# Three Strassen-like pairs instead of two in gate/up blocks 1 to 5, with two pairs' remainders built by adding transfers

## The chip, the cores and the metric

The kernel runs on one core of a Trainium2 chip. The metric is the device time of the program in microseconds (us). The engines are TensorE (PE; its weight loads are PEld), VectorE (DVE), ScalarE (ACT), GpSimd (POOL) and SyncE (SP, which here only issues transfers).

## The reference, cut to what matters

One decoder layer on 256 tokens of width 2048, in float32. The change touches only the first product of the two feed-forward parts.

```python
def swiglu(x, w_gate, w_up, w_down):
    return (jax.nn.silu(x @ w_gate) * (x @ w_up)) @ w_down
x = x + 0.5 * swiglu(rms_norm(x, ffn1_norm), ffn1_w_gate, ffn1_w_up, ffn1_w_down)   # D_FF = 5632
...  # attention and gated linear attention between two projections
x = x + 0.5 * swiglu(rms_norm(x, ffn2_norm), ffn2_w_gate, ffn2_w_up, ffn2_w_down)
```

## The kernel before, in words

**Numbers in two parts.** TensorE multiplies in a short format (fp32r). Every float32 operand W is therefore split: ACT copies it to `wh` (the rounded head), DVE subtracts `wl = W - wh` (the remainder). A product is three matmuls: head by head, remainder by head, head by remainder. The activations, `hh` and `hl`, are split once.

**Gate/up.** The 5632 columns go in 11 blocks of 512 gate and 512 up columns. In each, the 16 k-tiles of 128 rows come as eight *k-pairs*; a k-pair's weights are one transfer of 1 MB into a buffer `raw` (three buffers in rotation, issued on SP). A *plain* pair (letter `s`) costs 2 k-tiles x 2 token halves x 2 column groups x 3 = 24 matmuls of 128x512. A pair *by seven products* (letter `g`) uses Strassen's scheme with 7 products x 3 = 21 matmuls, and needs sums of weights, which DVE makes: `plain` (a sum and a split), `last` (`swh`, `swl`), `sums` (two additions, a split) and `more` (a split). `FF_ORDERS` gives the pairs' order: blocks 1 to 10 have `ssgssgss`, block 0 has `ssssssss`. The split weights lie in four buffers `wh`, `wl` (`WBUF`); `weights()` prepares up to three ahead.

**Around a block.** `evac` takes a block's results out of PSUM (two subtractions and additions `sg`, ACT's silu, a product `u`, a transpose `us`), and 32 small transfers on POOL's queue (`move_squares`, "moves") turn it. `finish`, which comes one block later, splits the turned result into `uh`, `ul`, the input of the down product. `fold` adds the seven-product banks together. `later` spreads such pieces over the plain pairs.

**What sets the order.** Each engine runs its own queue strictly in order. The queue is made at build time: a scheduler with a time model of its own reorders the program, so that it is not the order of the source.

Of the kernel before, what the change touches and what calls it, by code (L numbers as in the profile page):

```python
# [14 lines left out]
F32 = mybir.dt.float32  # L15
F32R = mybir.dt.float32r
U32 = mybir.dt.uint32
AF = mybir.ActivationFunctionType
ALU = mybir.AluOpType
AX = mybir.AxisListType  # L20

P = 128
S = 256
D = 2048
FF = 5632
# [5 lines left out]
FF_SEVEN = range(1, 11)  # L31
# [7 lines left out]
def _order(text):  # L39

    seven, plain = iter(range(text.count("g"))), iter(range(text.count("g"), len(text)))
    return [(next(seven), True) if c == "g" else (next(plain), False) for c in text]


FF_ORDERS = [_order("ssgssgss" if b in FF_SEVEN else "ssssssss") for b in range(FF // 512)]
DOWN_ORDERS = [_order("ssssssgssgssgsgsgsgsss"), _order("sgsssgssgssgssgsgsssss")]
OUT_ORDERS = [_order("ssssssss"), _order("ssgsgsss")]

# [1 line left out]
def layer_kernel(tc, x, xT, gains, gla_gate_up, gla_gate_bias, gla_out_norm, att_q_norm, att_k_norm,  # L50
                 w_ff1, w_dn1, w_mix, w_low, w_out, w_ff2, w_dn2, c_sq, c_rope, c_mask, out):

    nc = tc.nc
# [3 lines left out]
    with ExitStack() as es:  # L57
        cst = es.enter_context(tc.tile_pool(name="cst", bufs=1))
        wp = es.enter_context(tc.tile_pool(name="wp", bufs=2))
# [3 lines left out]
        order = [0]  # L63
# [109 lines left out]
            rsqrt(rt[:, t:t + 1], ssum[:, t:t + 1])  # L173


        def jobs_of(w, orders):
            for cp, order in enumerate(orders):
                for kp, seven in order:
                    for part in ("plain", "last", "sums", "more") if seven else (0, 1):
                        yield w, cp * len(order) + kp, part  # L180

        jobs = [*jobs_of(w_ff1, FF_ORDERS), *jobs_of(w_dn1, DOWN_ORDERS)]
        jobs += [(w_mix, i, k) for i in range(3 * KT // 2) for k in range(2)] + ["low"]
        jobs += [(w_mix, i, k) for i in range(3 * KT // 2, 3 * KT) for k in range(2)]
        jobs += jobs_of(w_out, OUT_ORDERS)
        jobs += [*jobs_of(w_ff2, FF_ORDERS), *jobs_of(w_dn2, DOWN_ORDERS)]

        AHEAD = 2
        ready = []
# [6 lines left out]
        def prepare():  # L196
            if not jobs:
                return
            job = jobs.pop(0)
            if job == "low":  # L200
                raw = wp.tile([P, KT, P], F32, name="raw", tag="raw", bufs=3)
                nc.sync.dma_start(raw, w_low.rearrange("p (k f) -> p k f", f=P))
                got = []
                for i in range(2):
                    w = wtile("wh").rearrange("p j f -> p (j f)").rearrange("p (k f) -> p k f", f=P)
                    nc.vector.memset(w.bitcast(F32), 0.0)
                    split(w[:, :, 0:RANK], w[:, :, 64:64 + RANK], raw[:, 8 * i:8 * i + 8, 0:RANK])
                    got.append(w)
                ready.extend(got)
                return  # L210
            w, i, k = job
            if k in ("last", "sums", "more"):
                return seven(k, w)
            if k == "plain" or k == 0:
                raw = raws[0] = wp.tile([P, 2, 2, 512], F32, name="raw", tag="raw", bufs=3)
                flat = raw.rearrange("p k j f -> p (k j f)")
                parts = 1 if started else 4
                started.append(True)
                for c in range(0, 2048, 2048 // parts):
                    nc.sync.dma_start(flat[:, c:c + 2048 // parts], w[i, :, c:c + 2048 // parts])  # L220
            if k == "plain":
                return seven(k, w)
            wh, wl = wtile("wh"), wtile("wl")
            if len(started) < 3:
                started.append(True)
                for j in range(2):
                    split(wh[:, j], wl[:, j], raws[0][:, k, j])
            else:
                split(wh, wl, raws[0][:, k])
            ready.append((wh, wl))  # L230

        rooms = {}

        def seven(part, w):

# [47 lines left out]
        later = []  # L283
# [45 lines left out]
        def seven_pair(acts, pairs, forms, odd, evac, fold, span=None, final=False):  # L329

            cs, ms, folds = [acc_bank(), acc_bank(), tp_bank(), tp_bank()] if odd is None else four_banks(odd), None, []
            if odd is not None:
                order[0] = 4 * (1 - odd)
            units = [u for kp, seven in pairs for u in ([kp] if seven else [(2 * kp,), (2 * kp + 1,)])]
            lastseven = max(n for n, u in enumerate(units) if not isinstance(u, tuple))
            steps = span or 2 * sum(isinstance(u, tuple) for u in units)
            total = done = step = n = 0  # L340
            while n < len(units):
                u = units[n]
                if isinstance(u, tuple):
                    g = WBUF if final and n == len(units) - WBUF else 1
                    ws = [weights() for _ in range(g)]
                    last = n + g == len(units)
                    for t in range(NT):
                        step += 1
                        total = max(total, done + len(later))
                        go = min(max(-(-total * min(step, steps) // steps) - done, 0), len(later))  # L350
                        done += go
                        run_later(go)
                        if folds:
                            folds.pop(0)()
                        now = [acts[v[0]] for v in units[n:n + g]]
                        products(cs[2 * t:2 * t + 2], t, now, ws, n == 0, last, ((0,), (1,)) if g > 1 else ((0, 1),))
                        if last:
                            evac(t, [c.rearrange("p (a b) -> p b a", b=2) for c in cs[2 * t:2 * t + 2]])
                    n += g
                    continue  # L360
                start = ms is None
                if start:
                    ms = [acc_bank() for _ in range(4)] if odd is None else four_banks(1 - odd)
                seven_products(cs, ms, acts[2 * u:2 * u + 2], forms[u], start, n == lastseven)
                if start:
                    later.extend(second)
                    second.clear()
                if n == lastseven:
                    folds = fold([m.rearrange("p (a b) -> p b a", b=2) for m in ms])
                    if holding[0] == 1:  # L370
                        later.extend(held)
                        held.clear()
                        holding[0] = total = done = step = 0
                        steps = 2 * (len(units) - n) - 6
                n += 1
# [35 lines left out]
        hacts = [(hh, hl, k) for k in range(KT)]  # L411

        def lent(a, k, i):

            return a[:, k:k + 2, :].rearrange("p k (t q) -> p (k t) q", q=P) if i else a[:, k:k + 2, :].rearrange("p k s -> p (k s)").unsqueeze(1)
# [15 lines left out]
        def ffn(name, done, residual, extra=None, final=False):  # L431

            with tc.tile_pool(name=name, bufs=1, reuse_waits="tile") as fp:

                tail = FT - TAIL
                us_h = [fp.tile([P, tail, S], F32R, name="uh")]
                us_l = [fp.tile([P, tail, S], F32R, name="ul")]
                spare = ExitStack()
                urs = xs[:, 0, 0:NT * 512].rearrange("p (t f) -> p t f", t=NT)
                extra_sums, tails = [], []  # L440

                def part(k):
# [3 lines left out]
                for b in range(FF // 512):  # L446
# [23 lines left out]
                    if b == FF_SEVEN[0]:  # L470
                        sp = spare.enter_context(tc.tile_pool(name=name + "s", bufs=1, reuse_waits="tile"))
                        t4 = xs[:, 1, :].rearrange("p (i f) -> p i f", i=4)
                        p1, u1, u2, u3 = [halves(t4[:, i, :]) for i in range(4)]
                        extra_sums = [u1, p1, u3, u2]
                        room = rooms["gate"] = {"sum": xs[:, 0, NT * 512:].rearrange("p (j f) -> p j f", j=2)}
                        for n in ("wh", "wl"):
                            room[n] = sp.tile([P, 1, 512], F32R, name="s" + n)
                        fs = [sp.tile([P, 2, 4, P], F32R, name="f" + n) for n in "hl"]
                        forms = {kp: [f[:, kp] for f in fs] for kp in range(2)}
                        later[:0] = [lambda kp=kp: seven_forms(hacts[2 * kp:2 * kp + 2], forms[kp], t4[:, 0, :], t4[:, 1, :]) for kp in range(2)]  # L480

                        def fold(m):
                            return [lambda: nc.scalar.activation(p1, m[0], AF.Copy),
                                    lambda: nc.vector.tensor_add(u1, p1, m[2]),
                                    lambda: nc.vector.tensor_add(u2, u1, m[3]),
                                    lambda: nc.vector.tensor_add(u1, u1, m[1]),
                                    lambda: nc.vector.tensor_add(u3, u2, m[1])]
# [500 lines left out]
```

## Time and profile before

| what | value |
|---|---|
| time, median of three runs (1716.45, 1719.28, 1719.43) | 1719.28 us |
| span of the profiled execution (the page gives no other time of it) | 1715.9 us |
| PE busy | 1705.4 us, 99% |
| DVE busy | 1416.9 us, 83% |
| ACT busy | 947.1 us, 55% |
| POOL busy | 505.7 us, 29% |
| moved by transfers | 378.62 MB, mean 221 GB/s |

The span runs from the first to the last instruction. A matmul's row shows 379 ns, since matmuls overlap in the pipeline; how fast they follow each other is read from two events whose matmuls are counted. Idle time of an engine other than PE costs something only where PE then waits.

### The profile page before, as it was taken

Reading aid. Unit: us, or ns where it says so; the run is one execution under the profiler, and the core shown is the slowest. Engines: PE = TensorE matmul, PEld = TensorE weight load, DVE = VectorE, ACT = ScalarE, POOL = GpSimd, SP = SyncE. Lnnn points to the kernel's source line nnn. Section 1 sums busy time; section 2 is a strip of 40 time slices with the busy share of each in tenths; the row PEclk is TensorE's granted clock in tenths of the full one; section 3 lists DMA queues with packets and bytes.
Section 4 is the critical chain, followed back from the end, with each engine's and each line's share of the span. In section 5 each row is a group of like instructions: output and inputs, shape, how many; then the busy total and the mean of one; then the engine's idle time right before and its main releaser. Section 6 shows DMA issues by size and latency. Waiting matters only on the chain.

```text
span 1715.9 us, 22309 instructions
## 1 busy us (share of the span) xinstructions
PE 1705.4 (99%) x7974; PEld 1485.1 (87%) x7974; DVE 1416.9 (83%) x1731; ACT 947.1 (55%) x1173; POOL 505.7 (29%) x1002
## 2 busy tenths in 40 slices
PE   9999999999999999999999999999999999999999
PEld 7888888888888888888888888888888888888887
DVE  6888889898898788577865788788888898898876
ACT  7555555555555555564654555555555555555453
POOL 0333334344410611054250043333333333420000
PEclk9999999999999999999999999999999999999999
DMA  8666666556665657577564467666666666665654
GB/s 345 213 229 224 219 211 232 208 213 236 234 250 219 217 203 244 192 237 235 195 210 172 148 198 269 210 231 225 222 224 220 226 212 224 218 242 222 248 204 147
DMA packets 85807, 378.62 MB, mean 221 GB/s; under 512 B 21392, under 2 KB 38800, under 8 KB 42688
## 3 DMA queue, kind: packets, MB, share of 16 engines
q1 hardware_dynamic: 50864, 350.25, 57.2%
q0 software_dynamic: 34112, 25.88, 5.3%
q8 instruction: 62, 1.02, 0.2%
q10 hardware_dynamic: 720, 1.07, 0.2%
q14 instruction: 49, 0.40, 0.1%
HBM read 354.57 MB, written 4.19 MB: 209 GB/s over the span
## 4 chain that ended last, share of the span: by engine, by line
PE 89%; DMA 4%; DVE 4%; POOL 1%; issue 1%; ACT 0%; DVEq 0%; SPq 0%; ACTq 0%; POOLq 0%
PE acc L279 20%; PE acc L277 20%; PE acc L281 20%; PE tp L281 4%; PE tp L277 4%; PE tp L279 4%; PE acc L303 4%; PE acc L304 4%; PE acc L302 4%; DVE wl L115 2%; DMA raw<-in_w_dn_dram 2%; DMA hh<-us 1%; PE tp L303 1%; PE tp L304 1%; PE tp L302 1%
## 5 line engine op out<-in xcount | busy, mean ns | idle before, releaser
L114 ACT ACTIVATE wh<-raw 128x1024 fp32r<-128x1024 f32 (+1 forms) x660 | 683.6, 1048 | 531.2 <-PE acc L281 186.6
L115 DVE TENSOR_TENSOR wl<-raw,wh 128x1024 fp32r<-128x1024 f32 (+1 forms) x658 | 790.3, 1215 | 168.4 <-ACT wh L114 165.0
L136 POOL DMA_DIRECT2D xs<-us x704 | 344.9, 497 | 552.1 <-ACT wh L114 200.3
L281 PE MATMUL acc<-wh,hl 128*128 128x512 f32 x1232 | 370.7, 380 | 0.0
L279 PE MATMUL acc<-wl,hh 128*128 128x512 f32 x1232 | 369.9, 380 | 0.1
L277 PE MATMUL acc<-wh,hh 128*128 128x512 f32 x1232 | 363.5, 381 | 2.6 <-ACT wh L114 2.6
L277 PEld LDWEIGHTS acc<-wh,hh 128*128 128x128 f32 x1232 | 232.3, 189 | 37.7 <-ACT wh L114 4.1
L279 PEld LDWEIGHTS acc<-wl,hh 128*128 128x128 f32 x1232 | 232.6, 189 | 33.9 <-issue 0.7
L281 PEld LDWEIGHTS acc<-wh,hl 128*128 128x128 f32 x1232 | 232.6, 189 | 32.9 <-DVE hl L544 0.2
L279 PE MATMUL acc<-wl,uh 128*128 128x512 f32 x384 | 117.2, 380 | 0.0
L281 PE MATMUL acc<-wh,ul 128*128 128x512 f32 x384 | 117.0, 379 | 0.0
L277 PE MATMUL acc<-wh,uh 128*128 128x512 f32 x384 | 112.1, 380 | 0.7 <-ACT wh L114 0.7
L136 POOL DMA_DIRECT2D hh<-us x128 | 62.4, 506 | 126.7 <-DVE us L129 69.0
L241 DVE TENSOR_TENSOR xs<-raw 128x1024 f32<-128x1024 f32 x40 | 49.0, 1225 | 46.9 <-DMA raw<-in_w_ff_dram 46.9
L277 PEld LDWEIGHTS acc<-wh,uh 128*128 128x128 f32 x384 | 72.3, 189 | 12.0 <-ACT wh L114 1.9
L279 PEld LDWEIGHTS acc<-wl,uh 128*128 128x128 f32 x384 | 72.4, 189 | 10.8 <-DVE wl L115 0.6
L281 PEld LDWEIGHTS acc<-wh,ul 128*128 128x128 f32 x384 | 72.6, 189 | 10.3
L277 PE MATMUL tp<-wh,hh 128*128 128x512 f32 x240 | 73.2, 379 | 0.0
L281 PE MATMUL tp<-wh,hl 128*128 128x512 f32 x240 | 71.4, 379 | 0.0
L279 PE MATMUL tp<-wl,hh 128*128 128x512 f32 x240 | 71.4, 379 | 0.0
L114 ACT ACTIVATE wh<-xs 128x1024 fp32r<-128x1024 f32 x40 | 42.2, 1055 | 45.2 <-PE acc L281 24.1
L114 ACT ACTIVATE swh<-raw 128x512 fp32r<-128x512 f32 x40 | 25.3, 631 | 60.6 <-DMA raw<-in_w_ff_dram 60.6
(326 smaller groups left out, 2382.3 us busy)
## 6 DMA issues: line engine op xcount, KB each, us to landing
raw<-in_w_ff_dram SPq DMA_DIRECT2D x175, 1024.0 KB, 5.0
raw<-in_w_dn_dram SPq DMA_DIRECT2D x88, 1024.0 KB, 4.9
raw<-in_w_mix_dram SPq DMA_DIRECT2D x48, 1024.0 KB, 5.0
raw<-in_w_out_dram SPq DMA_DIRECT2D x16, 1024.0 KB, 4.8
xs<-us POOLq DMA_DIRECT2D x704, 16.0 KB, 3.4
xs<-in_x_dram SPq DMA_DIRECT2D x2, 1024.0 KB, 9.8
xs<-in_x_dram POOLq DMA_DIRECT2D x2, 1024.0 KB, 5.4
hh<-us POOLq DMA_DIRECT2D x128, 16.0 KB, 3.7
```

What stands on the lines that cost most here:

```text
L114: nc.scalar.activation(dst_h, src, AF.Copy)
L115: nc.vector.tensor_sub(dst_l, src, dst_h.bitcast(F32))
L136: nc.gpsimd.dma_start(dst[32 * q:32 * q + 32, ..., r * n:(r + 1) * n], src[32 * r:32 * r + 32, ..., q * n:(q + 1) * n])
L241: nc.vector.tensor_add(room["sum"], b1, mid)
L277: nc.tensor.matmul(ps[j], lhsT=sh, rhs=alt(wh[:, j, :]), start=first and i == 0, stop=False)
L279: nc.tensor.matmul(ps[j], lhsT=sh, rhs=alt(wl[:, j, :]), start=False, stop=False)
L281: nc.tensor.matmul(ps[j], lhsT=sl, rhs=alt(wh[:, j, :]), start=False, stop=last and i == len(ws) - 1)
L302: nc.tensor.matmul(bank, lhsT=a[0], rhs=alt(ws[0][:, j, :]), start=start, stop=False)
L303: nc.tensor.matmul(bank, lhsT=a[0], rhs=alt(ws[1][:, j, :]), start=False, stop=False)
L304: nc.tensor.matmul(bank, lhsT=a[1], rhs=alt(ws[0][:, j, :]), start=False, stop=stop)
```

## The change

Blocks 1 to 5 of both gate/up products get the order `dsggdgss`: three pairs by seven products, three plain ones, and two of a new kind, `d`. A `d` pair's split is made in the previous block. A new job `far` loads the pair into `raw` as usual, ACT copies the heads `wh` and then writes `-wh` into the place of the remainder; a job `add` lets a transfer on POOL's queue add W from HBM onto it, so that `-wh + W` stands there. `take` hands the pair to the matmuls. The room for it is lent by `uh` and `ul`, k-tiles 24 to 39, which are filled only from block 6's results on; the forms of the third seven-product pair lie in k-tiles 20 and 21.

```diff
-FF_ORDERS = [_order("ssgssgss" if b in FF_SEVEN else "ssssssss") for b in range(FF // 512)]
+FF_FAR = range(1, 6)
+FF_ORDERS = [_order("dsggdgss" if b in FF_FAR else "ssgssgss" if b in FF_SEVEN else "ssssssss") for b in range(FF // 512)]
...
+        for b in FF_FAR:
+            for d, (at, to) in enumerate((((b - 1, 4), (b - 1, 6)), ((b - 1, 7), (b, 1)))):
+                ff_early.setdefault(at, []).append((b, d, "far"))
+                ff_early.setdefault(to, []).append((b, d, "add"))
...
+            if isinstance(k, str) and k[:4] == "take":
+                wh, wl = far[i]
+                ready.append((wh[:, int(k[4])], wl[:, int(k[4])]))
+                return
+            if isinstance(k, str) and k[:3] == "add":
+                nc.gpsimd.dma_start(far[i][1].rearrange("p k j f -> p (k j f)"), w[i], accum_op=ALU.add)
+                return
+            if isinstance(k, str) and k[:3] == "far":
+                raw = wp.tile([P, 2, 2, 512], F32, name="raw", tag="raw", bufs=3)
+                nc.sync.dma_start(raw.rearrange("p k j f -> p (k j f)"), w[i])
+                wh, wl = far[i] = [a.rearrange("p (k j h) s -> p k j (h s)", k=2, j=2) for a in rooms["far"][int(k[3])]]
+                for h in range(2):
+                    nc.scalar.activation(wh[:, h], raw[:, h], AF.Copy)
+                for h in range(2):
+                    nc.scalar.activation(wl[:, h], wh[:, h].bitcast(F32), AF.Copy, scale=-1.0)
+                return
...
+                rooms["far"] = [[a[0][:, k:k + 8, :] for a in (us_h, us_l)] for k in (24, 32)]
...
-                        forms = {kp: [f[:, kp] for f in fs] for kp in range(2)}
+                        forms[2] = [lent(a[0], 20, 1) for a in (us_h, us_l)]
```

The queues move with it. Line numbers after the change are 24 to 26 higher than before (L114 and L115 become L115 and L116, L241 becomes L265); L234 is the far head's copy, L236 the `-wh` copy, L231 the far load, L227 the add.

ACT's queue in block 3 of the first product before, from the silu of block 2's evac (`sg`) to the `finish` in the block's second half (`uh`; `wh<-xs` and `swh` belong to the `g` pairs):

```order
L452 ACTIVATE sg<-sg,rt 128x512
L114 ACTIVATE wh<-raw 128x1024
L114 ACTIVATE uh<-xs 128x4x128
L114 ACTIVATE wh<-raw 128x1024
L114 ACTIVATE wh<-xs 128x1024
L452 ACTIVATE sg<-sg,rt 128x512
L114 ACTIVATE wh<-raw 128x1024 x5
L114 ACTIVATE swh<-raw 128x512
L114 ACTIVATE wh<-raw 128x1024
L114 ACTIVATE wh<-xs 128x1024
L114 ACTIVATE wh<-raw 128x1024
L114 ACTIVATE uh<-xs 128x4x128
```

The same stretch after. The third row is the first `g`'s `more` copy, the fifth the second `g`'s `plain`, and the row `x2` below the second `g`'s `more` and the third `g`'s `plain`:

```order
L477 ACTIVATE sg<-sg,rt 128x512 x2
L234 ACTIVATE uh<-raw 128x1024 x2
L115 ACTIVATE wh<-raw 128x1024
L236 ACTIVATE ul<-uh 128x1024 x2
L115 ACTIVATE wh<-raw 128x1024
L115 ACTIVATE wh<-xs 128x1024
L115 ACTIVATE swh<-raw 128x512
L115 ACTIVATE wh<-raw 128x1024 x2
L115 ACTIVATE wh<-xs 128x1024
L115 ACTIVATE swh<-raw 128x512
L234 ACTIVATE uh<-raw 128x1024 x2
L115 ACTIVATE uh<-xs 128x4x128
```

Four copies of the first far pair now stand between the silu and the second `g`'s `plain`; two of the second far pair and a `finish` stand ahead of the third `g`'s `more` and the next plain pair, which come right behind the last row. So it is in blocks 1, 3 and 4 of the first product and 2, 3 and 4 of the second; in block 2 and block 1, respectively, the second far pair's copies stand behind the third `g`'s `more` and the first half of the plain pair. Block 5 has no far copies.

DVE's queue at the start of block 3 before, from the first `sg` of block 2's evac to the second one:

```order
L451 TENSOR_TENSOR sg<-acc,xs 128x512
L115 TENSOR_TENSOR wl<-raw,wh 128x1024
L453 TENSOR_TENSOR xs<-acc,xs 128x512 x2
L115 TENSOR_TENSOR wl<-raw,wh 128x1024
L454 SCALAR_TENSOR_TENSOR u<-xs,rt,sg 128x512
L115 TENSOR_TENSOR ul<-xs,uh 128x4x128
L129 STREAM_TRANSPOSE us<-u 128x4x4x32
L451 TENSOR_TENSOR sg<-acc,xs 128x512
```

And the same stretch after:

```order
L476 TENSOR_TENSOR sg<-acc,xs 128x512
L478 TENSOR_TENSOR xs<-acc,xs 128x512 x2
L273 TENSOR_TENSOR raw<-xs,raw 128x512
L116 TENSOR_TENSOR wl<-xs,wh 128x1024
L479 SCALAR_TENSOR_TENSOR u<-xs,rt,sg 128x512
L273 TENSOR_TENSOR raw<-raw 128x512
L265 TENSOR_TENSOR xs<-raw 128x1024
L130 STREAM_TRANSPOSE us<-u 128x4x4x32
L476 TENSOR_TENSOR sg<-acc,xs 128x512
```

The plain pairs' remainders that stood between the pieces of the evac have given way to the sums of the first `g` and the first addition of the second.

SP's queue in that region was one row of 81 equal loads; now far loads stand in it, and they take the same three buffers:

```order
L231 DMA raw<-in_w_ff_dram 128x2048
L244 DMA raw<-in_w_ff_dram 128x2048 x4
L231 DMA raw<-in_w_ff_dram 128x2048
L244 DMA raw<-in_w_ff_dram 128x2048 x2
L231 DMA raw<-in_w_ff_dram 128x2048
```

In block 3 the second far load waits for the buffer of the second `g`, which is free after that `g`'s last split. On POOL the adds stand in pairs, each pair behind one block's 32 moves and ahead of the next block's.

More of the change, by code (lines that the diff above doesn't have):

```diff
@@ L41, in _order @@
     seven, plain = iter(range(text.count("g"))), iter(range(text.count("g"), len(text)))
-    return [(next(seven), True) if c == "g" else (next(plain), False) for c in text]
-FF_ORDERS = [_order("ssgssgss" if b in FF_SEVEN else "ssssssss") for b in range(FF // 512)]
+    return [(next(seven if c == "g" else plain), c) for c in text]
+FF_FAR = range(1, 6)
+FF_ORDERS = [_order("dsggdgss" if b in FF_FAR else "ssgssgss" if b in FF_SEVEN else "ssssssss") for b in range(FF // 512)]
 DOWN_ORDERS = [_order("ssssssgssgssgsgsgsgsss"), _order("sgsssgssgssgssgsgsssss")]
@@ L173, in norm_finish, with jobs_of @@
             rsqrt(rt[:, t:t + 1], ssum[:, t:t + 1])
-        def jobs_of(w, orders):
+        def jobs_of(w, orders, early={}):
             for cp, order in enumerate(orders):
-                for kp, seven in order:
-                    for part in ("plain", "last", "sums", "more") if seven else (0, 1):
+                for at, (kp, kind) in enumerate(order):
+                    for b, d, part in early.get((cp, at), ()):
+                        yield w, b * len(order) + [k for k, c in orders[b] if c == "d"][d], part + str(d)
+                    for part in {"g": ("plain", "last", "sums", "more"), "s": (0, 1), "d": ("take0", "take1")}[kind]:
                         yield w, cp * len(order) + kp, part
-        jobs = [*jobs_of(w_ff1, FF_ORDERS), *jobs_of(w_dn1, DOWN_ORDERS)]
+        ff_early = {}
+        for b in FF_FAR:
+            for d, (at, to) in enumerate((((b - 1, 4), (b - 1, 6)), ((b - 1, 7), (b, 1)))):
+                ff_early.setdefault(at, []).append((b, d, "far"))
+                ff_early.setdefault(to, []).append((b, d, "add"))
+        jobs = [*jobs_of(w_ff1, FF_ORDERS, ff_early), *jobs_of(w_dn1, DOWN_ORDERS)]
         jobs += [(w_mix, i, k) for i in range(3 * KT // 2) for k in range(2)] + ["low"]
@@ L185, in layer_kernel @@
         jobs += jobs_of(w_out, OUT_ORDERS)
-        jobs += [*jobs_of(w_ff2, FF_ORDERS), *jobs_of(w_dn2, DOWN_ORDERS)]
+        jobs += [*jobs_of(w_ff2, FF_ORDERS, ff_early), *jobs_of(w_dn2, DOWN_ORDERS)]
         AHEAD = 2
@@ L230, in prepare @@
             ready.append((wh, wl))
-        rooms = {}
+        rooms, far = {}, {}
         def seven(part, w):
@@ L336, in seven_pair @@
                 order[0] = 4 * (1 - odd)
-            units = [u for kp, seven in pairs for u in ([kp] if seven else [(2 * kp,), (2 * kp + 1,)])]
+            units = [u for kp, kind in pairs for u in ([kp] if kind == "g" else [(2 * kp,), (2 * kp + 1,)])]
             lastseven = max(n for n, u in enumerate(units) if not isinstance(u, tuple))
@@ L479, in ffn @@
                         forms = {kp: [f[:, kp] for f in fs] for kp in range(2)}
-                        later[:0] = [lambda kp=kp: seven_forms(hacts[2 * kp:2 * kp + 2], forms[kp], t4[:, 0, :], t4[:, 1, :]) for kp in range(2)]
+                        forms[2] = [lent(a[0], 20, 1) for a in (us_h, us_l)]
+                        later[:0] = [lambda kp=kp: seven_forms(hacts[2 * kp:2 * kp + 2], forms[kp], t4[:, 0, :], t4[:, 1, :]) for kp in range(3)]
                         def fold(m):
```

## The prediction

> **What bounds the kernel now.** First the page's share of the span by engine, then busy time by stage: a stretch of gate/up blocks (50 to 90, 250 to 290) and one of the first down product (500 to 540). After the window stand span of the stretch, busy time (instructions) of PE, PEld, DVE, ACT, POOL, then granted clock, share of the transfer engines, GB/s.
>
> ```profile
> PE 1705.4 (99%) x7974; PEld 1485.1 (87%) x7974; DVE 1416.9 (83%) x1731; ACT 947.1 (55%) x1173; POOL 505.7 (29%) x1002
> 50.00:90.00 40.00, 40.00 (x187) 35.03 (x186) 33.03 (x36) 21.83 (x25) 15.76 (x32) 1.00 0.64 223
> 250.00:290.00 40.00, 40.00 (x187) 35.02 (x186) 35.74 (x41) 22.66 (x26) 15.69 (x32) 1.00 0.65 224
> 500.00:540.00 40.00, 38.69 (x177) 32.92 (x176) 34.34 (x36) 24.25 (x27) 0.00 (x0) 1.00 0.55 208
> ```
>
> In gate/up PE never stops, at full clock. DVE stands at 35.7 of 40 us there. Why it doesn't hold PE back is read from the timeline of ACT and DVE (start, duration, operation, and in brackets the idle time ahead of it) and from the waits between 50 and 250 us (sum, times, longest).
>
> ```profile
> 88.62 0.63 ACT L114 ACTIVATE swh<-raw 128x512 fp32r<-128x512 f32 x1 [1.75 <-DMA raw<-in_w_ff_dram]
> 100.56 3.21 ACT L114 ACTIVATE wh<-raw 128x1024 fp32r<-128x1024 f32 x3 [1.69 <-DVE raw L249]
> 114.29 1.07 ACT L114 ACTIVATE wh<-raw 128x1024 fp32r<-128x1024 f32 x1 [2.11 <-DVE raw L249]
> 128.71 0.63 ACT L114 ACTIVATE swh<-raw 128x512 fp32r<-128x512 f32 x1 [1.69 <-DMA raw<-in_w_ff_dram]
> 118.64 0.38 PE L302 MATMUL tp<-wh,fh 128*128 128x512 f32 x1
> 90.97 0.68 DVE L451 TENSOR_TENSOR sg<-acc,xs 128x512 f32<-128x512 f32 x1
> 91.57 0.68 DVE L453 TENSOR_TENSOR xs<-acc,xs 128x512 f32<-128x512 f32 x1
> 101.78 3.46 DVE L115 TENSOR_TENSOR wl<-raw,wh 128x1024 fp32r<-128x1024 f32 x3
> ACT wh L114 <- PE tp L281: 20.7, 18, 1.6
> ACT wh L114 <- PE acc L281: 13.7, 11, 1.5
> DVE wl L115 <- ACT wh L114: 11.9, 21, 1.3
> raw<-in_w_ff_dram SPq DMA_DIRECT2D x40, 1024.0 KB, 4.9
> ```
>
> The two `swh` rows are the same step one block apart: 40.09 us for 6 x 24 + 2 x 21 = 186 matmuls, so 0.2155 us each. ACT waits for PE to free a buffer (20.7 and 13.7 us): the preparation is as far ahead as four buffers let it. The second `g`'s `more` is ready on ACT at 115.36 and PE takes it at 118.64, 3.3 us later. That lead is what the change draws on. The other rows give prices: DVE starts 128x512 operations 0.60 us apart and takes 1.15 for 128x1024; ACT takes 1.07 for 128x1024; a load lands 4.9 us after its issue.
>
> **The change part by part.** *Matmuls.* Per changed block one plain pair becomes one by seven products: 3 matmuls less, in 10 blocks 30, on the path: 30 x 0.2155 = 6.5 us, or 40.09 to 39.44 us a block.
>
> *DVE.* A block loses the remainders of three plain pairs (6 x 1.15 = 6.9) and gains one `g`: four 128x1024 (4.6) and three 128x512 (1.8). It saves 0.5 us and is left with about 35.2 of 39.44, so sums alone show no loss. The third pair's forms come once a product, beside the plain block 0: nothing, covered by PE's queue of plain pairs.
>
> *ACT.* A block gains eight far copies (8.6) and one `swh` (0.6) and loses three long heads net (six of plain pairs fewer, three of the new `g` more; 3.2): +6.0 us, on an engine with 22.7 of 40 busy. By sum it is free. By order it is not, since ACT's queue runs strictly in turn. I walk one block (block 3, the kind that six of the eight blocks with far copies are), from the moment DVE starts the first `sg` of the last block's evac, with the prices above (0.62 for a mean 128x512 on DVE, 0.6 on ACT).
>
> - DVE does eight short and two long operations up to the second `sg`: 7.2. ACT stands with the silu until then, then does it (7.9), two far heads (10.0), the first `g`'s `more` (11.1), two `-wh` (13.2), the second `g`'s `plain` (14.2). DVE has two short pieces until 9.2, waits for `more` 1.9, and for `plain` 2.0.
> - The second `g`: DVE's three long and three short until 19.5, a wait of 1.1 for ACT's `more`, its remainder at 21.7. Only now is the buffer free for the second far load, which lands at 26.6.
> - Meanwhile the third `g`'s `plain`, `sums`, `last` and two additions: DVE is done at 25.8. ACT stands before the far load until 26.6, copies two heads (28.7), does a `finish` (29.3) and only then the third `g`'s `more` (30.4) and the plain pair's first half (31.4). PE comes for that `more` 125 matmuls into the block, at 26.9 plus 0.65 of a first wait for `sg`: 27.6. It waits 2.8 there and 0.6 for the plain half.
> - DVE's remainder ends at 31.5. Up to the next first `sg` it has eight long and five short operations (12.2) and 0.5 of waits: 44.2.
>
> So the period of such a block is 44.2 us against 40.1, with 9 us of DVE idle beside 35.2 busy. Were the far load to land by the time PE has left the old far pair (24.3), it would be 41.9; this is the lower end. For the two blocks whose far heads stand behind the third `g`'s `more`, the same walk gives 43.0, by a wait of 3.5 for the four far copies in front. Block 5 has no far copies: 39.44.
>
> *The loads.* The 20 far loads replace 20 plain loads of the same size; only their place is new, and is in the walk. *The adds* are 20 new transfers of 1 MB. No row shows one that adds. The nearest rows are POOL's plain loads and the two loads on SP in the crowded start:
>
> ```profile
> xs<-in_x_dram POOLq DMA_DIRECT2D x2, 1024.0 KB, 5.4
> xs<-in_x_dram SPq DMA_DIRECT2D x2, 1024.0 KB, 9.8
> 98.07 8.80 POOL L136 DMA_DIRECT2D xs<-us  x18 [26.21 <-ACT wh L114]
> 118.12 0.50 POOL L136 DMA_DIRECT2D xs<-us  x1 [0.28 <-DMA xs<-us]
> q1 hardware_dynamic: 5747, 41.84, 59.3%
> ```
>
> POOL issues a block's 32 moves from 7.1 us after the first `sg` (90.97) to 118.6. The first add stands behind them, 27.6 us into the block, and PE wants it at 39.4 or later. With 5.4 to 9.8 us of landing it costs PE nothing, and below nothing is excluded, since nothing waits for less. The second has over 15 us. The moves behind the adds may start some us later; their `finish` stands over 18 us behind. What the adds can cost is the landing of other loads: 41.84 MB took 59.3% of 200 us, 2.8 us a MB; two more MB a block raise 26 of 40 to 31.3 of 39.4 if an add is like a load, so I take nothing, with an upper end of 4.9 us (9.8 less 4.9) a block, for the one load that DVE waits for in the last step of the walk.
>
> The Trainium skill (Collectives: The Full Stack, "The bandwidth ceiling: the fold count and why AG ≠ RS ≠ AR") says that a transfer that adds makes two source reads, and so halves its rate. By this an add would take 5.6 us a MB instead of 2.8, the share would be 37 of 39.4, and the upper end the likelier; no run here shows it yet.
>
> *Sum.* First product: block 1 enters with DVE ahead, 44.2 less the 1.4 that the lag takes to build, +2.7; block 2 +2.9; blocks 3 and 4 +4.1 each; block 5 -0.65: +13.2. Second product: block 1 half of 2.9, three times +4.1, -0.65: +13.1. Upper end +26.3. With 41.9 in place of 44.2 (+1.8 six times, less the same 1.4) the sum is +12.5. I take the middle, +20: the walk has the far load land late everywhere, but each us that PE waits elsewhere brings it nearer to the lower end. On the profiled span of 1715.9 that is 1736; the median of the runs is 3.4 above that span, so 1739.
>
> **The rivals.** *Faster: the waits don't form.* If in a block the third `g`'s `more` is ready within 27.6 us of the walk's start, which needs the second far load to land 2.8 us earlier than I have it (a load is issued earlier because DVE keeps the lead of four buffers it has now), PE never stops, and all that stays is 30 matmuls: 1719.3 - 6.5 = 1713. For it speaks that DVE's sum falls; against it, that DVE already idles for ACT 11.9 us in 200 when ACT has no far copies.
>
> *Mild.* The down product has as dense a run of `g` pairs with DVE at 34.3 busy, and PE lost 1.3 of 40 us there. Eight blocks at 1.3 make +10.4, less 6.5: +4, 1723. Against it: no foreign copies stand in ACT's queue there.
>
> *Adds crowd the loads.* 2 to 4.9 us more in eight blocks, on top of +20: 1755 to 1778. *The adds are late themselves:* from 12 us of landing on, PE waits for the first add at each block's head; each us costs 9 us in all. It ends in the same place, and I count it here.
>
> **How the numbers follow.** Walk 0.48, no waits 0.24, mild 0.15, crowding 0.13. Predicted: the walk, 1739, its own range 1731 to 1746. The range for 8 in 10 takes in the faster case and the middle of the gap to crowding: 1712 to 1762. A measurement of this kernel can tell about 0.2%, 3.4 us, from no change. Faster 0.24; same, half of mild, 0.08; slower 0.68.
>
> **What would show it.** Right: PE idle of 2 to 4 us in blocks 1 to 4 ahead of the third `g`'s `more` and the plain pair, released by ACT, while ACT waits ahead of a far copy for a load; DVE busy near 35 in stretches of 42 to 44 us. Wrong: PE at 40.00 of 40 in these blocks (no waits); PE waiting for an add (late adds); weights' loads landing well over 4.9 us (crowding).

## The result, and the profile after

The changed kernel takes 1826.84 us (median of 4 runs) against 1718.96: a ratio of 1.0629, 95% interval 1.0614 to 1.0644, slower by 108 us. That is far outside the predicted 1712 to 1762. The profiled execution has a span of 1821.8 us, 105.9 more than before.

Page line of the busy time, then by window (columns as above), first product's blocks 1 to 5 in the first four rows, then two later stretches (the four are windows of 40 us, not one row a block):

```profile
PE 1728.8 (95%) x7944; PEld 1494.1 (82%) x7944; DVE 1418.4 (78%) x1755; ACT 993.7 (55%) x1235; POOL 524.7 (29%) x1022
50.00:90.00 40.00, 36.18 (x165) 30.45 (x164) 33.72 (x38) 29.39 (x34) 18.44 (x35) 1.00 0.78 244
90.00:130.00 40.00, 28.80 (x125) 24.21 (x124) 26.15 (x31) 18.19 (x21) 14.74 (x31) 0.87 0.64 205
170.00:210.00 40.00, 31.67 (x135) 26.49 (x135) 26.55 (x30) 21.42 (x26) 10.57 (x20) 0.91 0.78 236
250.00:290.00 40.00, 29.30 (x126) 25.02 (x126) 26.51 (x32) 14.70 (x18) 15.70 (x32) 0.87 0.52 171
290.00:330.00 40.00, 40.00 (x187) 35.08 (x186) 36.54 (x42) 23.41 (x27) 15.16 (x31) 1.00 0.62 223
500.00:540.00 40.00, 40.00 (x186) 34.87 (x185) 34.73 (x60) 20.81 (x25) 16.20 (x33) 1.00 0.59 214
```

PE stands idle up to 11 of 40 us in the changed blocks and, but for one place told below, nowhere else. No engine is the bound there: between 90 and 130 us DVE is busy 26 of 40, ACT 18. Even the granted clock falls, to 0.87. From block 6 on (row 290) all is as before. So the time goes into waits. These are the waits between 50 and 310 us (sum, times, longest), and two transfers with their median landing:

```profile
PE acc L326 <- DVE sg L476: 35.7, 4, 10.8
ACT swh L115 <- DMA raw<-in_w_ff_dram: 19.5, 5, 5.9
ACT wh L115 <- DMA raw<-in_w_ff_dram: 18.0, 6, 7.1
DVE xs L265 <- DMA raw<-in_w_ff_dram: 17.6, 6, 4.9
raw<-in_w_ff_dram SPq DMA_DIRECT2D x41, 1024.0 KB, 6.0
ul<-in_w_ff_dram POOLq DMA_DIRECT2D x9, 1024.0 KB, 12.3
```

PE waits four times, once at the head of each of blocks 2 to 5, for `sg`, the instruction that empties the last block's banks. DVE and ACT are late with it because they wait for weights. One such head, in order of time: the adds on POOL, ACT, DVE, PE (start, duration, idle time ahead in brackets), and from the chain of waits the load behind it.

```profile
82.21 0.95 POOL L227 DMA_DIRECT2D ul<-in_w_ff_dram  x1
87.43 0.85 POOL L227 DMA_DIRECT2D ul<-in_w_ff_dram  x1 [4.26 <-ACT ul L236]
```

```profile
96.12 2.00 ACT L115 ACTIVATE wh<-raw 128x1024 fp32r<-128x1024 f32 x2 [7.10 <-DMA raw<-in_w_ff_dram]
97.20 2.36 DVE L116 TENSOR_TENSOR wl<-raw,wh 128x1024 fp32r<-128x1024 f32 x2 [5.80 <-ACT wh L115]
102.81 1.23 DVE L265 TENSOR_TENSOR xs<-raw 128x1024 f32<-128x1024 f32 x1 [3.25 <-DMA raw<-in_w_ff_dram]
105.69 0.69 DVE L476 TENSOR_TENSOR sg<-acc,xs 128x512 f32<-128x512 f32 x1
106.52 0.76 PE L326 MATMUL acc<-wh,hh 128*128 128x512 f32 x1 [10.83 <-DVE sg L476]
```

```profile
87.36 15.43 DMA raw<-in_w_ff_dram
102.81 1.23 DVE xs L265
```

The two adds are issued at 82.2 and 87.4. A load issued at 87.36 lands only after 15.43 us, where such loads took 4.9 before. The last plain pair's copy and the next `g`'s sum wait for late loads, and `sg` stands behind them in DVE's queue. PE has nothing from 95.7 to 106.5. How busy the transfer engines were then (last two columns: share, GB/s; the one ahead is the granted clock): first the kernel before around the same block boundary, then the changed kernel as a whole and in pieces, and its two queues between 88 and 92 us (packets, MB, share of 16 engines):

```profile
76.00:96.00 20.00, 20.00 (x95) 17.50 (x94) 16.94 (x20) 11.54 (x13) 0.00 (x0) 1.00 0.61 211
84.00:104.00 20.00, 11.69 (x55) 9.90 (x53) 10.85 (x13) 8.21 (x11) 0.85 (x1) 0.90 1.02 297
84.00:88.00 4.00, 4.00 (x21) 3.50 (x20) 3.90 (x6) 4.00 (x7) 0.57 (x1) 1.00 1.03 266
92.00:96.00 4.00, 3.69 (x18) 2.88 (x16) 0.00 (x0) 0.00 (x0) 0.00 (x0) 1.00 1.03 285
96.00:100.00 4.00, 0.00 (x0) 0.00 (x0) 2.36 (x2) 2.00 (x2) 0.00 (x0) 1.00 1.05 287
100.00:104.00 4.00, 0.00 (x0) 0.00 (x0) 1.19 (x2) 1.19 (x2) 0.00 (x0) 0.52 0.98 373
104.00:108.00 4.00, 1.48 (x4) 1.23 (x5) 4.00 (x7) 2.58 (x4) 0.00 (x0) 0.50 0.63 264
q0 software_dynamic: 68, 0.56, 66.9%
q1 hardware_dynamic: 67, 0.55, 34.0%
```

For 20 us the transfer engines are full, where they were busy 0.61 before. The queue of the adds (q0) takes 66.9% of 16 x 4 us for 68 packets, 0.63 us each; the loads' queue (q1) 34.0% for 67, 0.32 us each. A transfer of 1 MB is 128 packets of 8 KB, so an add takes all 16 engines for about 5 us, a load for 2.6.

One loss lies outside the changed blocks, in the second product's block 0, where the first far pair is fetched (ACT, then PE):

```profile
1107.26 2.00 ACT L234 ACTIVATE uh<-raw 128x1024 fp32r<-128x1024 f32 x2 [5.58 <-DMA raw<-in_w_ff_dram]
1108.36 1.22 PE L301 MATMUL acc<-uh,hh 128*128 128x512 f32 x2 [4.35 <-ACT uh L234]
1111.72 1.22 PE L301 MATMUL acc<-wh,hh 128*128 128x512 f32 x2 [2.14 <-ACT hh L115]
```

That far load is issued at 1101.86 us and ACT stands before it; the last split of the activations (`hh`) waits behind the far copies.

Where each kernel lost time, in us against before, from the starts of its matmuls counted from either end. The experiments are told below; "sevens" is the number of seven-product pairs in a changed block, and 30 matmuls less (6.5 us; 27 in e13) are already in the numbers with three. Each row is one profiled execution (those of e2 and e10 are 3.8 us above their kernels' medians); the columns miss the end by up to 4 us, which lie elsewhere, up to 2.2 of them ahead of the first product's block 1.

| kernel | sevens; far pairs; transfers behind them | first product, blocks 1 to 5 | second, block 0 | second, blocks 1 to 5 | end |
|---|---|---|---|---|---|
| changed | 3; 2; 1 MB adding | 52.8 | 10.2 | 42.6 | 105.9 |
| e1 | 3; 2; 1 MB plain | 28.3 | 10.1 | 25.2 | 63.3 |
| e2 | 3; 2; 16 KB adding | 8.9 | 8.5 | 1.1 | 21.2 |
| e3 | 3; 2; none, DVE | 0.0 | 6.5 | 9.5 | 17.7 |
| e6 | 3; 1; 1 MB adding | 29.3 | 10.3 | 30.4 | 71.2 |
| e7 | 3; 0; none | 12.9 | 0.0 | 12.4 | 25.1 |
| e8 | 2; 2; 1 MB adding | 40.9 | 9.0 | 35.3 | 84.6 |
| e10 | 2; 2; 16 KB adding | 0.0 | 9.2 | 1.0 | 14.2 |
| e11 | 2; 2; 1 MB plain | 17.0 | 10.0 | 15.3 | 40.3 |
| e12 | 3; 2; 1 MB adding, moved | 18.8 | 2.7 | 27.5 | 50.7 |
| e13 | 3; 2; none, DVE; second product from block 2 | 0.8 | 0.0 | 7.2 | 6.4 |

### The profile page after: what moved, and what is told of

Same layout as the page of the kernel before. It is cut to its first block, busy times and chain, and to the rows that moved or that the text cites. A ratio compares the mean times of both kernels' runs of the same rounds, so it can differ in the third digit from the quotient of the medians.

```text
span 1821.8 us, 22378 instructions
## 1 busy us (share of the span) xinstructions
PE 1728.8 (95%) x7944; PEld 1494.1 (82%) x7944; DVE 1418.4 (78%) x1755; ACT 993.7 (55%) x1235; POOL 524.7 (29%) x1022
## 4 chain that ended last, share of the span: by engine, by line
PE 74%; DMA 12%; DVE 6%; issue 3%; POOL 2%; ACT 2%; DVEq 0%; SPq 0%; ACTq 0%; POOLq 0%
PE acc L303 16%; PE acc L305 16%; PE acc L301 16%; DMA raw<-in_w_ff_dram 5%; PE acc L326 4%; PE acc L327 4%; PE acc L328 4%; PE tp L303 3%; PE tp L305 3%; PE tp L301 3%; DVE wl L116 3%; DMA xs<-us 3%; POOL xs L137 2%; DMA ul<-in_w_ff_dram 1%; DMA hh<-us 1%
## 5 line engine op out<-in xcount | busy, mean ns | idle before, releaser
L115 ACT ACTIVATE wh<-raw 128x1024 fp32r<-128x1024 f32 (+1 forms) x620 | 637.9, 1047 | 512.6 <-PE acc L305 168.9
L116 DVE TENSOR_TENSOR wl<-raw,wh 128x1024 fp32r<-128x1024 f32 (+1 forms) x618 | 741.3, 1217 | 222.0 <-ACT wh L115 219.6
L301 PE MATMUL acc<-wh,hh 128*128 128x512 f32 x1064 | 314.9, 384 | 8.2 <-ACT wh L115 5.8
L303 PE MATMUL acc<-wl,hh 128*128 128x512 f32 x1064 | 321.6, 382 | 0.3
L305 PE MATMUL acc<-wh,hl 128*128 128x512 f32 x1064 | 321.8, 382 | 0.0
L303 PEld LDWEIGHTS acc<-wl,hh 128*128 128x128 f32 x1064 | 201.4, 190 | 30.8 <-DVE wl L116 2.0
L305 PEld LDWEIGHTS acc<-wh,hl 128*128 128x128 f32 x1064 | 201.7, 190 | 28.4 <-DVE hl L570 0.2
L326 PE MATMUL acc<-wh,hh 128*128 128x512 f32 x142 | 56.0, 401 | 62.6 <-DVE sg L476 62.6
L265 DVE TENSOR_TENSOR xs<-raw 128x1024 f32<-128x1024 f32 x50 | 61.2, 1224 | 57.0 <-DMA raw<-in_w_ff_dram 57.0
L305 PEld LDWEIGHTS acc<-wh,ul 128*128 128x128 f32 x384 | 72.7, 189 | 10.2
L234 ACT ACTIVATE uh<-raw 128x1024 fp32r<-128x1024 f32 x40 | 40.6, 1048 | 53.1 <-DMA raw<-in_w_ff_dram 37.7
L115 ACT ACTIVATE swh<-raw 128x512 fp32r<-128x512 f32 x50 | 31.3, 625 | 66.0 <-DMA raw<-in_w_ff_dram 65.4
L115 ACT ACTIVATE wh<-xs 128x1024 fp32r<-128x1024 f32 x50 | 52.4, 1048 | 26.6 <-PE acc L305 16.8
```

The lines of the kernel that those rows point to most:

```text
L115: nc.scalar.activation(dst_h, src, AF.Copy)
L116: nc.vector.tensor_sub(dst_l, src, dst_h.bitcast(F32))
L234: nc.scalar.activation(wh[:, h], raw[:, h], AF.Copy)
L265: nc.vector.tensor_add(room["sum"], b1, mid)
L301: nc.tensor.matmul(ps[j], lhsT=sh, rhs=alt(wh[:, j, :]), start=first and i == 0, stop=False)
L303: nc.tensor.matmul(ps[j], lhsT=sh, rhs=alt(wl[:, j, :]), start=False, stop=False)
```

## The experiments

Theory A: the adding transfers fill the transfer engines, the weights' loads come late, and PE waits. Theory B: the order of far copies and far loads on ACT makes the waits, as the predicted walk had it. Theory C came up later: it is the place of the adds that costs.

**The addition alone (e1).** The order on every queue is the changed kernel's, and the bytes are the same.

```
-  nc.gpsimd.dma_start(far[i][1]..., w[i], accum_op=ALU.add)
+  nc.gpsimd.dma_start(far[i][1]..., w[i].bitcast(F32R))
```

> Left out: the addition; the 20 adding transfers write W over -Wh instead (same 1 MB, same queue, same place in every queue; the remainders are wrong). Theory A (an adding transfer holds the transfer engines about twice as long as a plain one: 8 KB packets 0.63 us against 0.31 in the changed kernel's trace, so that the two adds at each block's end push the weights' loads to 13 to 15 us): packets of these transfers fall to 0.31 us, the loads at the block's end land in 6 to 9 us, the head-of-block waits of PE (6.5 to 10.8 us) fall below 4, time 1730 to 1770. Theory B (the order of ACT and of the far loads makes the waits, as the walk had it; the addition as such costs nothing): less than 15 us of the 108 go, 1810 to 1830.

Measured: 1783.01 us, ratio 1.039 (1.0368 to 1.0411). The two queues in its crowded stretch (84 to 96 us), its longest PE waits between 46 and 300 us, and the landing of its plain and `g` loads between 40 and 300 us:

```profile
q1 hardware_dynamic: 409, 3.09, 62.2%
q0 software_dynamic: 270, 1.95, 40.6%
PE acc L326 <- DVE sg L476: 16.0, 4, 4.4
DMA to landing us min/median/max: 4.7/5.4/9.6
```

A MB on q0 now takes 40.6% x 192 us / 1.95 = 40 engine-us, against 66.9% x 64 / 0.56 = 76 with the addition. The head waits fall from 35.7 to 16.0 us. So 44 of the 108 us are the addition as such, 2.2 for each of 20 transfers. Theory A's direction holds, its 1730 to 1770 doesn't: a plain MB at that place still costs. B as stated, by which less than 15 us would go, is out; how the 65 us that are left divide between the plain bytes and the order, this run can't tell.

**Nearly no bytes (e2).** The same transfers cut to `[:, 0:32]`.

> Left out: all but 32 of 2048 columns of each adding transfer (16 KB instead of 1 MB; the remainders are wrong); the scheduler, which prices transfers by size, orders the queues anew. Far loads, far copies and the third seven-product pair stay. Theory A: without the transfers' time the loads land in about 5 us, no head-of-block wait above 3 us, 1712 to 1745. Theory B: the walk's waits stay, 1735 to 1830.

Measured: 1735.15, ratio 1.0105 (1.0082 to 1.0127). The time lies in A's range and on the lower edge of B's (1735), so it alone doesn't choose; that no wait for `sg` is left speaks for A. 48 us more go with the bytes, though the order changed too, so part of them may be the order's. What stays has B's form. ACT and PE in block 2 of the first product:

```profile
121.42 2.00 ACT L234 ACTIVATE uh<-raw 128x1024 fp32r<-128x1024 f32 x2 [4.45 <-DMA raw<-in_w_ff_dram]
123.33 1.99 ACT L115 ACTIVATE wh<-raw 128x1024 fp32r<-128x1024 f32 x2
124.42 0.79 PE L326 MATMUL tp<-wh,uh 128*128 128x512 f32 x1 [3.20 <-ACT wh L115]
```

ACT stands before the second far load, the third `g`'s `more` comes behind it, and PE waits 3.20 us. It is one of three such waits in e2; the others are 2.57 us in the first product and 2.00 in the second.

**The remainder by DVE (e3), and no far pairs (e7).**

```
 e3: -  nc.scalar.activation(wl[:, h], wh[:, h].bitcast(F32), AF.Copy, scale=-1.0)   (and no add)
     +  nc.vector.tensor_sub(wl[:, h], raw[:, h], wh[:, h].bitcast(F32))
 e7: -  "dsggdgss"      +  "ssggsgss"      (no far, no add)
```

> The far pairs stay, but DVE subtracts their remainders from the raw load in place of the ACT's four negated copies and the adding transfers; the result is complete. DVE gets 4 x 1.15 = 4.6 us a block more, 39.8 of 39.44 to be had, ACT 4.3 less. Theory A: the loss goes with the adds, what is left is DVE's bound: 10 blocks at 0 to 3 us over the 40.1 of before, 1718 to 1750. Theory B (late far loads and their copies hold ACT, and through it DVE): 1750 to 1800.

> No far pairs: blocks 1 to 5 have ssggsgss, three pairs by seven products and five plain, all split as before; 30 matmuls less. DVE sum 35.7 + 6.4 - 2.3 = 39.8 of 39.44 a block. Theory A and B both: DVE is the bound, 0.4 us a block if nothing else waits (1719 - 6.5 + 4 = 1717), up to 3 us a block by waits for ACT: 1715 to 1750. It tells what the far pairs had to relieve.

Measured: e3 1735.48, ratio 1.0111 (1.0087 to 1.0135); e7 1741.76, ratio 1.0146 (1.0127 to 1.0164). e3 lies in A's range and below B's. Both are near DVE's bound, as expected: between 50 and 290 us DVE is busy 38.3 of 40 us in e3 and 36.5 in e7. With the far pairs split early, the first product's five blocks come out even (0.0 in the table), without them they lose 12.9. The far pairs do relieve; the transfers that were to spare DVE 4.6 us a block cost twice as much (91 us over ten blocks between e3 and the changed kernel, which differ in ACT's negated copies and in the order, too).

**Two sevens, and one far pair (e8, e6).** Orders `dsgsdgss` and `dsggsgss`; in e6 only the first far pair and its add stay.

> Blocks 1 to 5 have dsgsdgss: the two far pairs and their 20 adding transfers stay, the third pair by seven products goes back to a plain one (no matmul saved; DVE 31 of 40 us, ACT about 27). Theory A1 (two adding transfers a block are too much for the transfer engines beside the loads, whatever DVE and ACT have to do): loads at a block's end still land in 10 us or more, PE waits at each block's head, 1755 to 1800. Theory A2 (they hurt because with three sevens DVE and ACT have no lead to lose): the loads land as late, but PE waits below 2 us a block, 1718 to 1740.

> Blocks 1 to 5 have dsggsgss: one far pair instead of two, so 10 adding transfers in all, one a block, and still three pairs by seven products (30 matmuls less). DVE 37.5 of 39.4 us a block. Theory A (two adds back to back are what makes the loads late; one takes 5 us of the engines by its packets): loads land in 9 us at most, head waits below 3 us, 1725 to 1760. Rival (any add at the block's end meets the loads): half of the loss or more stays, 1765 to 1790.

Measured: e8 1804.58, ratio 1.0505 (1.0487 to 1.0523); e6 1789.53, ratio 1.0416 (1.0401 to 1.0432). In e8 DVE has much slack (22 to 31 of 40 us busy), and PE waits all the same (block 2's head; landing of the plain and `g` loads):

```profile
101.64 0.76 PE L326 MATMUL acc<-wh,hh 128*128 128x512 f32 x1 [7.39 <-DVE sg L476]
DMA to landing us min/median/max: 4.7/5.4/14.0
```

A2 is out, and the time is slightly above A1's range. In e6 theory A was wrong on the time and the rival right: although loads there land within 8.4 us and no wait for `sg` is over 3.1, 48 us more than in e7 are lost with 10 adds. About 10 of these are the far load's in the second product's block 0, which e7 doesn't have. The other 34 in blocks 1 to 5 show that one far pair with its add, without a second add beside it, costs PE time; no run has e6 without its adds, so the adds' part of the 34 is not shown.

**Two sevens with small and with plain transfers (e10, e11).** The same two edits as in e2 and e1, on e8.

> The kernel with two far pairs and two sevens (dsgsdgss), with adding transfers of 16 KB instead of 1 MB (left out: the rest of the addition, the remainders are wrong); the scheduler orders anew. Theory A (each 1 MB adding transfer costs PE about 4.3 us however much lead DVE and ACT have): what stays is the wait in the second product's block 0 (about 9 us, a far load without a free buffer, in every far kernel so far), and nothing in blocks 1 to 5: 1722 to 1735. Rival (the far copies and loads themselves cost): over 1745.

> The same with the transfers writing W plainly over -Wh (left out: the addition), 1 MB each; the order on every queue is that of the adding kernel with two sevens. Theory A: a plain transfer takes half the packet time, so about half of the 75 us that its blocks 1 to 5 lost: 1755 to 1780. Rival (the write as such, not the packets' time): 1790 to 1805.

Measured: e10 1728.13, ratio 1.0058 (1.0038 to 1.0078); e11 1758.95, ratio 1.024 (1.0224 to 1.0256). Both lie in theory A's ranges and outside the rivals'. A stretch in e8 and the same in e10 (far pairs, far copies, 10 small adds; nothing lost):

```profile
90.00:130.00 40.00, 32.24 (x141) 27.20 (x140) 24.66 (x29) 21.07 (x24) 16.68 (x33) 0.91 0.74 235
...
90.00:130.00 40.00, 40.00 (x187) 34.96 (x186) 31.25 (x37) 26.11 (x30) 17.56 (x34) 1.00 0.65 235
```

The first row is e8's, the last e10's. PE's wait for `sg` between 46 and 300 us (sum, times, longest), e8's and then e11's:

```profile
PE acc L326 <- DVE sg L476: 23.2, 4, 7.4
PE acc L326 <- DVE sg L476: 6.4, 2, 5.0
```

This is the clean price: e8 to e11, in the same order on all queues, 45.6 us or 2.3 an add for the addition; e11 to e10, in another order, 30.8 or 1.5 for the plain MB. The difference in packet time is 128 packets x (0.63 - 0.32) / 16 = 2.5 us a transfer. With two sevens, far copies and far loads cost next to nothing in blocks 1 to 5 (0.0 and 1.0 us).

**The place (e9, e12).** e9 brings both far pairs forward, e12 the first alone:

```
 changed: (((b - 1, 4), (b - 1, 6)), ((b - 1, 7), (b, 1)))
 e9:      (((b - 1, 1), (b - 1, 2)), ((b - 1, 5), (b - 1, 6)))
 e12:     (((b - 1, 2), (b - 1, 3)), ((b - 1, 7), (b, 1)))
```

> The far pairs are written 3 and 2 places earlier in the list of jobs (far at places 1 and 5, add at 2 and 6 of the block before, instead of 4 and 7, 6 and the next block's 1); all work stays, the scheduler orders anew, the adds still stand in pairs between two blocks' moves. Theory A (sum of the transfers: they take 10 us of 40 more wherever they stand): 1800 to 1840. Theory C (place: only the meeting with the loads of the block's end costs): 1740 to 1790.

> The changed kernel with the first far pair of a block brought 2 places earlier in the block before (far at place 2, add at place 3 instead of 4 and 6); the second pair stays. The result is complete. An add of the next block then stands with the second add of this block, ahead of a block's moves instead of behind them. Theory A (amount): 1810 to 1845. Theory C (place: the adds hurt because they meet the loads at the block's end): 1760 to 1795.

e9 ran 1784.02, but tells nothing on place, and its expectation was mistaken to say that all work stays as it was: places 1 and 5 lie ahead of the old pair's last matmuls in program order, so these read the next block's pair and wait for it. e12 keeps the program's meaning: 1771.61, ratio 1.0312 (1.0291 to 1.0334). POOL's two adds there, and PE's largest sum of waits between 46 and 300 us:

```profile
88.80 0.91 POOL L227 DMA_DIRECT2D ul<-in_w_ff_dram  x1 [2.96 <-ACT ul L236]
101.82 0.87 POOL L227 DMA_DIRECT2D ul<-in_w_ff_dram  x1 [12.10 <-ACT ul L236]
PE acc L327 <- DVE wl L116: 6.2, 7, 1.3
```

With 13 us between the two adds instead of 5.2 the long head waits of the first product are gone, and 55 us with them, at the same 20 MB (in the second product one stall of 11.6 us stays). So theory C holds for half of the loss, and A's "amount" fails as the whole. Which of the new order's effects does it, the spacing or which loads are met, wasn't separated.

**Without the second product's block 0, and the first product alone (e13, e14).** e3 with far pairs from block 2 on in the second product; then with none there.

> The kernel with remainders by DVE and no adds, with the second product's far pairs in blocks 2 to 5 only (block 1 as before: ssgssgss, 3 matmuls more). If the far load in the second product's block 0 is what costs 6.5 us there, these go, and block 1's share of the second product's remaining 9.5 us: 1735.5 - 6.5 - 2 = 1727, range 1723 to 1731. If not: 1733 to 1738.

> The kernel with remainders by DVE and no adds, with the third seven-product pair and the far pairs in the first product only; the second product's blocks as before. In the second product none of the 6 us lost there by the last kernel; in the first 15 matmuls less (3.2 us) and waits that took about as much (it stood 0.7 us behind before at its end): 1717 to 1721, no change. If the third pair were a gain once the adds are gone: 1714 to 1716.

Measured: e13 1725.03, ratio 1.0043 (1.0029 to 1.0057): the loss in block 0 is the far load's. e14 1717.67 against 1718.06, ratio 0.9997 (0.9988 to 1.0006): no change. None of the kernels beats the one before; the third seven-product pair is worth, at best, what its waits take back.

## Why the prediction was wrong, point by point

- *Matmuls:* right. 7944 against 7974; 6.5 us.
- *DVE and ACT:* near the sums, and neither bounds the changed blocks. DVE has 1418.4 us in all against 1416.9, where the sum had 5 less; ACT has 46.6 us more, where the sum had 60.
- *ACT's order and the walk:* the walk's wait is real but smaller and rarer than forecast. In the changed kernel PE waits 0.65 to 1.66 us for the third `g`'s `more` in three blocks of each product. In e2, without the adds' bytes, it waits 3.20, 2.57 and 2.00 us in three of the eight blocks with far copies; the walk had 2.8 in the kind of block that six of them are. It gave +26.3 with late far loads everywhere and +12.5 with early ones; e2's ten blocks came to +10.0 (8.9 + 1.1), just below the lower end. I took +20, twice too much. In e10, with one `g` less, it is nothing.
- *The adds:* the step that failed: "so I take nothing, with an upper end of 4.9 us (9.8 less 4.9) a block, for the one load that DVE waits for in the last step of the walk". The term put at nothing measured 92 us between the changed kernel and e2: 44 by the addition as such (e1, same order), 48 by the bytes and the new order that came with their going. Three things were mis-sized. An add takes the engines twice as long as a load (76 engine-us a MB against 40), and its own landing of 8.4 to 15.1 us lies above the 5.4 to 9.8 assumed. The busy share was taken over a block, 31.3 of 39.4, where it is the 20 us after the adds' issue that decide: they are full, as two adds (about 10 us of all engines) meet four loads (about 10 us). And not one load is late but several in a row, up to 10.5 us each.
- *Who waits for DVE at that place:* the walk began with DVE's first `sg` and took it as in time. It is this `sg` that comes late, and with it the bank that PE needs at the block's head: 6.5 to 10.8 us in each of blocks 2 to 5. The rival "adds crowd the loads" named the right cause, but with 2 to 4.9 us in eight blocks, 1755 to 1778 in all; measured were 9 to 14 us in four of the first product's five blocks.
- *The rule of the Trainium skill* (Collectives: The Full Stack, "The bandwidth ceiling: the fold count and why AG ≠ RS ≠ AR") that the add makes two source reads and halves the rate is told there of the reduce steps of ring collectives. It was weighed for these adds and left out of the sum. The trace agrees with the factor: 0.63 us a packet against 0.32. The two reads themselves no run here shows.
- *The start of the second product* was not looked at: 10.2 us in block 0, a term that was missing. "The 20 far loads replace 20 plain loads of the same size; only their place is new, and is in the walk" overlooked a far load with `hh` behind its copies.
- *"PE waiting for an add"* didn't occur; PE's rows name `sg` and ACT, not `ul`.

The sum in the measured terms, first product: counted from start to start of the matmuls, steps of over 0.9 us make 43.5 us beyond the 0.2155 each, slower matmuls and small gaps 12.5 more than before, 15 matmuls less take off 3.2: 52.8, as in the table.

## What to carry to other kernels

Price a transfer that adds at twice the engine time of a plain one, and set it against what the transfer engines carry in the same 10 to 20 us, not against their mean share: 64% busy left no room for two MB more beside four loads. Ask of each late load which instruction stands behind its consumer in the in-order queues; here it was the one that frees PE's banks. When work is fetched far ahead, look at the first block that has to fetch it, too.

## What the runs showed of the hardware

A stall of PE can cost more than its length: after most of the long ones the granted clock is half, and the matmuls that follow start 0.43 instead of 0.2155 us apart. Below, a stall of the changed kernel that did not do it (PE and the window around it), then the smallest that did:

```profile
82.39 0.48 PE L326 MATMUL acc<-wh,uh 128*128 128x512 f32 x1 [1.66 <-ACT wh L115]
80.00:84.00 4.00, 2.10 (x9) 1.21 (x8) 1.63 (x2) 4.00 (x5) 3.16 (x6) 1.00 0.42 109
187.75 0.48 PE L326 MATMUL acc<-wh,uh 128*128 128x512 f32 x1 [1.57 <-ACT wh L115]
188.69 1.08 PE L301 MATMUL acc<-wh,hh 128*128 128x512 f32 x2 [0.25 <-ACT wh L115]
186.00:189.00 3.00, 1.18 (x4) 0.60 (x4) 1.96 (x3) 3.00 (x5) 0.00 (x0) 0.98 0.95 232
189.00:192.00 3.00, 3.00 (x8) 2.34 (x8) 1.90 (x3) 2.96 (x4) 0.00 (x0) 0.50 0.91 330
192.00:195.00 3.00, 3.00 (x14) 2.58 (x14) 3.00 (x5) 2.00 (x2) 0.85 (x1) 0.95 1.05 322
```

Gaps of 1.57 and 0.25 us are followed by 3.4 us at half clock, in which 8 matmuls run in 3 us where 14 would; about 1.7 us more are lost. After the stalls of 6.5 to 10.8 us the half clock lasts 6.8 or 10.2 us, though part of it passes in the stall itself. The length of a gap alone doesn't decide: the gap of 1.66 us and one of 1.79 at 52 us left the clock at 1.00, and so did a stall of 3.63 us in e1 at 241 us. In the trace's clock records of the changed kernel the stretches at half clock last 3.41, 6.83 or 10.24 us, and those at full clock between them are whole multiples of 3.41, too (40.96 is 12, 13.65 is 4). Where a stall lies on this beat may be what decides; that was not tested. The Trainium skill (TensorE: Matmul & The Clock Gate, "Part 1: The HAM clock gate (the "warmup" mystery)") has windows of about 3.4 us and the halved clock after an idle one. The lengths agree with its 3.4; the 1.57 us that suffice here are shorter.
